# Layer 0's head in another fixed order: a hybrid decoder trunk on one core

## Chip, cores, metric

The kernel runs on one core of one Trainium2 chip. The metric is the device time of one execution in microseconds (us), as the median of several runs. The profile is one further execution, taken by the hardware profiler; its times count from the span's start.

## The reference

Two layers, each a mixing block and an MLP, on 512 positions of width 1024:

```
for l in range(2):
    h = rms_norm(x, norm_mix_g[l])
    proj = h @ w_in[l]                      # 1024 -> 26 groups of 128 columns
    mixed = [diff_attention(...), short_conv(...), rwkv7_time_mix(...)]
    x = x + mixed @ w_out[l]
    h = rms_norm(x, norm_mlp_g[l])
    x = x + square(relu(h @ w_mlp_up[l])) @ w_mlp_down[l]
return rms_norm(x, final_norm_g)
```

with `rms_norm(x, g) = x * rsqrt(mean(x*x) + 1e-6) * g`. Everything is float32.

## The kernel before, in words

**Layout.** Activations lie transposed: `x[j]`, j = 0 to 7, holds 128 channels by 512 positions. A weight group g is 128 output columns; its 1024 rows are eight blocks k of 128 x 128, loaded as halves of four blocks. A product on TensorE (PE) multiplies one block by one 128 x 512 tile into PSUM.

**Three products for one.** For precision each operand is split in a high part (rounded to fp32r) and a low part (the rest). Block k of group g takes three products: high weight by high input, high weight by low input, low weight by high input (`passes`, L685 ff.; all matmuls are issued from L282).

- The high part of input tile j, `ahim` in the profile, is made by ScalarE (ACT) from x[j] and the norm's gain (L420); the text calls it ahi j. Its low part, `alom`, is made by VectorE (DVE) after it (L421): alo j.
- The high part of a weight half, `whi` or `whi_s`, is a cast on ACT from the loaded tile `raw` (L671). The low part, `wlo` or `wlo_s`, is a subtraction on DVE or GpSimd (POOL) (L683). `raw` has three buffers; the next load waits for the low part of the tile that lay there.
- The norm works on x itself: the first square goes straight into the accumulator `accm` (L429), the later squares `sqm` (L433, ACT, two buffers) are added to it by DVE (L436): square j, sum j. PE then adds over the partitions (`pssm`, called pss here), DVE and POOL take the inverse root, PE spreads it over the partitions (`prbm`, called prb), ACT copies it to `rsm` (L789). The projections are scaled by `rsm` only after their products.

**The head.** In layer 0 the first three groups, 24, 18 and 15, go through the eight blocks together: for each k three products of each group, nine in all, so that PE can begin when input tile 0 and the first blocks are there. Their first halves are loaded and cast in two pieces (one block, then three). After the 72 products of the head come the other groups one by one, group 0 first. Group 24 feeds the rates (`rates`, L804 ff.): scaled by `rsm` (`pwa`), mixed with the position before (`dwa`, `zwa`), tanh (`th`), split in parts (`tw`, `to`), and then multiplied by small weights (`lkt`, `lvt` from the load `lor`) into `pw`, three times; a DVE scan (L835) takes each `pw` out of PSUM.

**What sets the order.** Nothing is scheduled by the compiler: `drive` walks through a string per layer, `ORDER[l]`. Each letter is a generator, and a letter with a number takes so many of its steps; a step issues one instruction or a few. So the string fixes the order on every engine and on every DMA queue. The letters of the changed stretch are: d the loads (SyncE's queue, SP, but for two), e ahi and alo, q squares and sums, w casts to high parts, x low parts on DVE, y low parts on POOL, m products, k constants (among them the cast `exact` of the load `ex`), n the norm from pss to `rsm`, g the rates. `SLOTS` fixes in the same way which buffer each new tile takes; the load `ex` takes its turn in the two buffers of the squares.

Of the kernel before, what the change touches and what calls it, by code (L numbers as in the profile page):

```python
# [56 lines left out]
      "xyxyyxxxyyxxyyxyxxyxyyxyyyyyyxxxyyyxyxyyyyyyyxxxxxyyyyyyyyyyxyxyxxxxyyxxyy")  # L57

ORDER = (
         "g d10 e w e m w x m w m x m2 x m q m3 w x e m w e m2 x m2 w x m d2 e m3 d3 e m3 q2 m3 d q2 e q e q d5 w2 e w x e x d4 m3 q2 x d2 m2 e m2 e "  # L60
         "d m2 q e m2 q m4 e k q m3 e m3 q2 m3 k4 q e k m5 k3 m7 n3 w y m2 w2 m2 x d2 m3 n2 g y m6 k g d k m3 k g2 m k2 m4 g m g m2 w m2 g m2 g x m3 "
         "d g5 m2 g2 m3 A w g m4 g y A2 d m4 A2 m3 g m2 g2 w m y h m6 R g3 d R2 g R m4 w m2 g m g4 y R m3 R d m R m2 A2 m h R2 m w m3 A x d A m2 A m "
         "R m A2 m R3 m2 A2 m2 R3 m w x m A m2 A m5 d m4 R3 w m4 x R2 m4 d m4 g2 R2 w A m A y A7 m2 d m A R4 A5 m11 w y R2 m A2 m d A2 m A m r A2 R r "
         "A m4 A3 m w y R2 r h A3 R9 r d r2 m3 A2 h2 R3 m A m A3 R m2 r A2 m2 r R3 m4 w m A3 m2 R r2 y R m5 A2 r2 R2 d A m A2 r m A m2 A r m3 r3 A B "
# [1543 lines left out]
```

## Time and profile before

| | us |
|---|---|
| median of 3 runs | 1241.8 |
| lowest, highest | 1240.58, 1242.72 |
| span of the profiled execution | 1241.5 |

The page gives the busy time of each engine over the span, the waits and the chain of work that ended last; the time line gives instructions with their start, duration, engine, line, output and inputs, and in brackets the idle time of the engine ahead of it and what ended that. The page names no time of the profiled execution but its span, from the first to the last instruction.

### The profile page before, as it was taken

What the parts mean: (1) busy time and instruction counts of PE and PEld (TensorE: products, weight loads), DVE (VectorE), ACT (ScalarE), POOL (GpSimd) and SP (SyncE); (2) the same over time, 40 slices, a digit from 0 to 9 for tenths busy, and PEclk for the clock granted to TensorE, in tenths of its full rate; (3) what the DMA queues carried; (4) which work ended last, traced back from release to release, by engine and by line L of the source; (5) the groups of instructions that cost most, each with busy time, mean ns of one, the idle gap of its engine ahead of it and who ended that gap; (6) DMA issues with size and microseconds to landing.
All of it is one profiled execution on the core that took longest, in us unless ns stands there. A gap on an engine that the chain in (4) does not pass through costs nothing.

```text
span 1241.5 us, 24974 instructions
## 1 busy us (share of the span) xinstructions
PE 1230.0 (99%) x9492; PEld 1055.0 (85%) x9492; DVE 912.1 (73%) x1776; ACT 675.0 (54%) x1410; POOL 368.0 (30%) x457
## 2 busy tenths in 40 slices
PE   9999999999999999999999999999999999999997
PEld 6888888888899998989887888888888999998987
DVE  6787888868767676765766777887687767676753
ACT  6785655548445454544464657464583445454542
POOL 1263637342311111111026355464231211111111
PEclk9999999999999999999999999999999999999999
DMA  6523324142433333321235244332433333333121
GB/s 216 163 87 99 105 96 111 53 153 85 136 102 98 107 94 106 99 85 44 69 106 164 79 118 119 89 83 73 158 102 120 102 102 98 107 94 107 55 68 68
DMA packets 84695, 127.90 MB, mean 103 GB/s; under 512 B 21472, under 2 KB 25568, under 8 KB 84576
## 3 DMA queue, kind: packets, MB, share of 16 engines
q1 hardware_dynamic: 83568, 125.64, 33.1%
q8 instruction: 74, 1.21, 0.4%
q10 hardware_dynamic: 1008, 0.68, 0.2%
q14 instruction: 45, 0.37, 0.1%
HBM read 117.11 MB, written 9.18 MB: 102 GB/s over the span
## 4 chain that ended last, share of the span: by engine, by line
PE 93%; ACT 2%; DVE 2%; DMA 1%; POOL 1%; issue 1%; ACTq 0%; POOLq 0%; DVEq 0%
PE dn L282 25%; PE pj L282 20%; PE pa L282 11%; PE po L282 8%; PE up L282 7%; PE pb L282 6%; PE dnF L282 4%; PE pc L282 3%; PE sc L282 1%; DMA raw<-wts 1%; PE ptt L287 1%; PE pg L282 1%; PE pyy L282 1%; PE pzw L282 1%; PE pst L282 1%
## 5 line engine op out<-in xcount | busy, mean ns | idle before, releaser
L1392 POOL TENSOR_TENSOR ml<-m,mh 128x512 fp32r<-128x512 f32 x64 | 108.9, 1716 | 481.0 <-ACT mh L1391 340.6
L344 ACT CAST whi<-raw 128x512 fp32r<-128x512 f32 x142 | 87.4, 619 | 162.4 <-PE dn L282 152.8
L282 PE MATMUL dn<-mh,whi 128*128 128x512 f32 x448 | 174.8, 390 | 0.1
L282 PE MATMUL dn<-ml,whi 128*128 128x512 f32 x448 | 174.6, 390 | 0.0
L282 PE MATMUL dn<-mh,wlo 128*128 128x512 f32 x448 | 174.5, 390 | 0.0
L683 POOL TENSOR_TENSOR wlo<-raw,whi 128x512 fp32r<-128x512 f32 x84 | 111.0, 1321 | 213.1 <-ACT whi L671 175.4
L282 PE MATMUL pj<-ahim,whi 128*128 128x512 f32 x392 | 156.7, 400 | 0.4 <-DVE vf L1278 0.4
L282 PE MATMUL pj<-ahim,wlo 128*128 128x512 f32 x392 | 156.4, 399 | 0.0
L282 PE MATMUL pj<-alom,whi 128*128 128x512 f32 x392 | 155.9, 398 | 0.0
L1516 DVE TENSOR_TENSOR x<-dn,x 128x512 f32<-128x512 f32 x112 | 77.3, 690 | 103.1 <-PE dn L282 103.1
L671 ACT CAST whi<-raw 128x512 fp32r<-128x512 f32 x142 | 87.6, 617 | 83.3 <-PE pj L282 25.1
L345 DVE TENSOR_TENSOR wlo<-raw,whi 128x512 fp32r<-128x512 f32 x142 | 115.0, 811 | 11.2 <-ACT whi L344 8.3
L282 PEld LDWEIGHTS dn<-mh,wlo 128*128 128x128 f32 x448 | 84.1, 188 | 17.8
L282 PEld LDWEIGHTS dn<-mh,whi 128*128 128x128 f32 x448 | 84.1, 188 | 17.5 <-issue 0.4
L282 PEld LDWEIGHTS dn<-ml,whi 128*128 128x128 f32 x448 | 84.1, 188 | 16.7
L1455 ACT CAST shi_p<-s 128x512 fp32r<-128x512 f32 x96 | 59.6, 621 | 70.1 <-PE pa L282 55.1
L282 PEld LDWEIGHTS pj<-ahim,whi 128*128 128x128 f32 x392 | 73.9, 188 | 14.1 <-issue 0.8
L282 PEld LDWEIGHTS pj<-alom,whi 128*128 128x128 f32 x392 | 73.9, 188 | 13.9 <-issue 0.5
L282 PEld LDWEIGHTS pj<-ahim,wlo 128*128 128x128 f32 x392 | 73.9, 188 | 13.8 <-issue 0.2
L1456 DVE TENSOR_TENSOR slo_p<-s,shi_p 128x512 fp32r<-128x512 f32 x96 | 67.9, 708 | 19.7 <-ACT shi_p L1455 17.2
L282 PE MATMUL pa<-tlo,shi_p 128*128 128x256 f32 x288 | 81.3, 282 | 0.0
L282 PE MATMUL pa<-thi,shi_p 128*128 128x256 f32 x288 | 81.2, 282 | 0.0
(414 smaller groups left out, 3208.1 us busy)
## 6 DMA issues: line engine op xcount, KB each, us to landing
raw<-wts SPq DMA_DIRECT2D x389, 256.0 KB, 2.7
qs<-dqhi SPq DMA_DIRECT2D x24, 128.0 KB, 3.7
ks<-dkhi SPq DMA_DIRECT2D x24, 128.0 KB, 3.7
x<-xT SPq DMA_DIRECT2D x8, 256.0 KB, 4.6
dqhi<-qhi SPq DMA_DIRECT2D x6, 256.0 KB, 3.4
dqlo<-qlo SPq DMA_DIRECT2D x6, 256.0 KB, 3.4
dkhi<-khi SPq DMA_DIRECT2D x6, 256.0 KB, 2.7
dklo<-klo SPq DMA_DIRECT2D x6, 256.0 KB, 3.5
```

Source lines behind the costliest of these rows:

```text
L282: ins = nc.tensor.matmul(*a, **k)
L287: ins = nc.tensor.transpose(*a, **k)
L344: act.copy(hi[:, :n], raw[:, :n])
L345: (pool if a and lean[0] else dve).tensor_tensor(lo[:, :n], raw[:, :n], hi[:, :n].bitcast(F32), ALU.subtract)
L671: yield act.copy(hi[:, k0:k1], raw[:, k0:k1])
L683: yield eng.tensor_tensor(lo[:, k0:k1], raw[:, k0:k1], hi[:, k0:k1].bitcast(F32), ALU.subtract)
L1392: pool.tensor_tensor(lo, m, hi.bitcast(F32), ALU.subtract)
L1455: act.copy(hi, src)
L1456: dve.tensor_tensor(lo, src, hi.bitcast(F32), ALU.subtract)
L1516: dve.tensor_tensor(x[j], pt, x[j], ALU.add)
```

## The change

Two lines of the order of layer 0 are changed. The number of steps of each letter in them is the same before and after, and all lines behind them are untouched.

```diff
-"g d10 e w e m w x m w m x m2 x m q m3 w x e m w e m2 x m2 w x m d2 e m3 d3 e m3 q2 m3 d q2 e q e q d5 w2 e w x e x d4 m3 q2 x d2 m2 e m2 e "
-"d m2 q e m2 q m4 e k q m3 e m3 q2 m3 k4 q e k m5 k3 m7 n3 w y m2 w2 m2 x d2 m3 n2 g y m6 k g d k m3 k g2 m k2 m4 g m g m2 w m2 g m2 g x m3 "
+"g d10 e w e m w x m w m x m2 x m e m3 w e x m3 w x m2 w x m d2 e m3 d3 e q e m3 e q2 m3 d6 w e x e q w x w x e2 q2 d4 m3 q d2 m2 e m2 q "
+"d m2 e q m2 e m4 q k q m3 e m3 q2 m3 k4 q2 k m5 k3 m13 n3 w y m2 w2 m3 x d2 m3 n2 g y k g d k m2 k g2 m k2 m4 g m g m2 w m2 g m2 g x m3 "
```

Written out by engine:

- ACT, before: square 0, cast 24, ahi1, casts 18 and 15 (second pieces), ahi2, squares 1 and 2, ahi3, square 3, casts of the second halves of 24 and 18, ahi4, that of 15, square 4, ahi5, square 5, ahi6, exact, square 6, ahi7, square 7.
- ACT, after: ahi1, casts 24, 18 and 15 (second pieces), ahi2, square 0, ahi3, square 1, cast of the second half of 24, ahi4, square 2, those of 18 and 15, ahi5, square 3, ahi6, square 4, ahi7, square 5, exact, squares 6 and 7.
- DVE, after: alo1 ahead of the low part of 24's second piece; alo2, alo3, sum 1, low part of 24's second half, alo4, low parts of 18's and 15's, alo5, sums 2 and 3, alo6, sums 4 and 5, alo7, sum 6, four small constants, sum 7. Before, a sum stood behind each of alo2 to alo6 or close to it, and alo7 behind sum 7.
- PE: the products keep their order. pss stands six products later among them, and eight products instead of seven lie between pss and prb; so prb stands seven products later, and fewer products lie between prb and the first product into `pw`.
- The order on POOL and on SP's queue is the same.

## The prediction

> **What bounds the kernel now.** I read the page first, for the engine that never rests. TensorE (PE) is busy 99% of the span at full clock, and the chain that ended last is 93% PE. Time can only move where PE waits.
>
> ```profile
> span 1241.5 us, 24974 instructions
> PE 1230.0 (99%) x9492; PEld 1055.0 (85%) x9492; DVE 912.1 (73%) x1776; ACT 675.0 (54%) x1410; POOL 368.0 (30%) x457
> PE 93%; ACT 2%; DVE 2%; DMA 1%; POOL 1%; issue 1%; ACTq 0%; POOLq 0%; DVEq 0%
> ```
>
> The change touches the first 27 us, so the next views are the busy time by stretches (duration, then PE, PEld, DVE, ACT, POOL), and the chain in order of time.
>
> ```profile
> 0.00:22.00 22.00, 19.62 (x75) 12.74 (x75) 14.81 (x33) 15.68 (x30) 1.22 (x7) 1.00 0.82 268
> 22.00:45.00 23.00, 23.00 (x112) 18.95 (x112) 17.23 (x31) 17.41 (x30) 8.79 (x12) 1.00 0.33 104
> ```
>
> ```profile
> 6.57 0.53 ACT accm L429
> ...
> 8.83 0.56 DVE wlo_s L683
> ...
> 9.41 4.32 DMA raw<-wts
> ...
> 25.45 7.54 PE pj L282 x33
> ```
>
> PE idles some 2.4 us before 22 us and not at all from 22 to 45. The chain gives PE's pace: 7.54 / 33 = 0.228 us from product to product. It also shows what delays the start: the first square (accm), and a weight load that went out only at 9.41, when DVE had finished the low part of an earlier tile. The time line has PE's waits:
>
> ```profile
> 7.19 0.40 PE L282 MATMUL pj<-ahim,wlo_s 128*128 128x512 f32 x1
> 8.18 0.50 PE L282 MATMUL pj<-ahim,whi_s 128*128 128x512 f32 x1 [0.59 <-ACT ahim L420]
> 8.97 0.50 PE L282 MATMUL pj<-alom,whi_s 128*128 128x512 f32 x1 [0.29 <-DVE alom L421]
> 9.30 0.40 PE L282 MATMUL pj<-ahim,wlo_s 128*128 128x512 f32 x1
> 15.05 0.50 PE L282 MATMUL pj<-ahim,whi_s 128*128 128x512 f32 x1
> 20.25 0.39 PE L282 MATMUL pj<-ahim,whi_s 128*128 128x512 f32 x1
> 21.61 0.95 PE L282 MATMUL pssm<-ones,accm 128*128 128x1 f32 x8
> ```
>
> **First part, input tile 1 ahead of its square.** ACT and DVE around it:
>
> ```profile
> 6.48 0.63 ACT L429 ACTIVATE accm<-x 128x512 f32<-128x512 f32 x1
> 7.01 0.50 ACT L671 CAST whi_s<-raw 128x384 fp32r<-128x384 f32 x1
> 7.41 0.72 ACT L420 ACTIVATE ahim<-x,prm 128x512 fp32r<-128x512 f32 x1
> 8.16 0.75 DVE L421 SCALAR_TENSOR_TENSOR alom<-x,prm,ahim 128x512 fp32r<-128x512 f32 x1
> ```
>
> ahi1 takes the square's place: 6.48 + 0.72 = 7.20 (if tile 1 has landed by 6.48; ACT was busy, so the row can't show it, and at the worst ahi1 starts at 7.41 as now and the step gains nothing). Each instruction here starts some 0.1 before the end of the one ahead, so the cast behind it runs 7.10 to 7.60, and PE's first product of tile 1 starts at 7.64 instead of 8.18. alo1 follows ahi1: 7.23 to 7.98, so the second product starts at 8.03; the weight's low part follows 7.88 to 8.44, so the third starts at 8.49 against 9.30. That is 0.8 gained; I keep 0.75, since a product after a wait took 0.33, not 0.23, until the next.
>
> **Second part, tiles 4 to 7 ahead of squares and of late casts.** From 15.05 to 20.25 PE issued 18 products, 4.10 at its pace, in 5.20: 1.1 of waits, on alo4, the low part of weight 15's second half and alo5. ahi4 stood behind the cast that waited for the load of 9.41; the change puts ahi4 and alo4 before it. With tile 4 done by about 13.7 and the rest below, no product of tiles 4 to 6 finds its operand missing. So PE could be at the norm's sums (pss) 0.75 + 1.1 = 1.85 earlier. The change puts six products ahead of pss, 6 x 0.228 = 1.37: in the order of before pss would stand at 21.61 + 1.37 = 22.98, and PE now arrives at 22.98 - 1.85 = 21.1.
>
> **Third part, the sums.** pss needs all eight squares added by DVE, and these have been pushed back. Rows for the paces, and for the wait that now decides:
>
> ```profile
> 17.02 0.63 ACT L433 ACTIVATE sqm<-x 128x512 f32<-128x512 f32 x1 [0.37 <-DVE accm L436]
> 17.51 0.74 DVE L421 SCALAR_TENSOR_TENSOR alom<-x,prm,ahim 128x512 fp32r<-128x512 f32 x1
> 18.17 0.68 DVE L436 TENSOR_TENSOR accm<-accm,sqm 128x512 f32<-128x512 f32 x1
> 18.77 0.74 DVE L421 SCALAR_TENSOR_TENSOR alom<-x,prm,ahim 128x512 fp32r<-128x512 f32 x1
> 13.75 0.62 ACT L671 CAST whi_s<-raw 128x512 fp32r<-128x512 f32 x1 [1.46 <-DMA raw<-wts]
> 20.04 0.16 DVE L445 TENSOR_SCALAR drv<-prm 128x11 f32<-128x11 f32 x1
> 20.40 0.69 DVE L436 TENSOR_TENSOR accm<-accm,sqm 128x512 f32<-128x512 f32 x1
> ```
>
> DVE takes 0.66 from a low part to the next instruction and 0.60 from a sum. The squares share two buffers, so a square waits for the sum two allocations back: the 0.37 above.
>
> The load of 9.41 waits for the low part of 8.83, ended at 9.39; that now ends at 8.90 (two low parts of 0.56, started 0.47 apart, behind the one that ends at 8.44), so the cast of 13.75 starts at about 13.25. The next load's cast follows to 14.6, ahi5 to 15.2, alo5 15.25 to 16.0. Only then come sum 2 (15.9) and sum 3 (16.5 to 17.2). Square 4 has to wait for sum 3's buffer: 17.25 to 17.87. Sum 4 runs 17.9 to 18.6, square 5 in the same buffer 18.6 to 19.25, sum 5 19.27 to 19.95, alo7 from 19.87, sum 6 from 20.53, four small instructions (20.40 - 20.04 = 0.36), sum 7 from 21.5 to 22.2. pss then starts at 22.25, and PE, there since 21.1, waits 1.1: of the 1.85, 0.73 is left. If the load keeps its 13.75, everything is 0.45 later (pss 22.7); if it takes only the 2.7 of the last row below, ACT is what its cast waits for, 0.25 earlier (22.0).
>
> SP's queue has a part. ex shares the squares' buffers and now waits for sum 2, 16.6 instead of 13.79; queued behind it are four constant loads and the next weights. The cast named exact waits for ex, and squares 6 and 7 stand behind exact.
>
> ```profile
> 13.79 0.33 SPq L648 DMA_DIRECT2D ex<-cst  x1
> 16.47 18.09 SPq L629 DMA_DIRECT2D raw<-wts  x8
> 21.14 1.88 ACT L671 CAST whi<-raw 128x512 fp32r<-128x512 f32 x3 [0.77 <-DMA raw<-wts]
> ```
>
> ```profile
> ex<-cst SPq DMA_DIRECT2D x1, 128.0 KB, 3.5
> raw<-wts SPq DMA_DIRECT2D x1, 256.0 KB, 2.7
> ```
>
> A load from an empty queue took 2.7 (the one issued at 23.40), ex itself, behind others, 3.5. With 2.7 exact starts at 19.35, square 6 ends at 20.4, before sum 6 wants it: no cost. With 3.5 square 6 ends at 21.2, sum 6 starts at 21.23 and pss at 22.95. I take 2.7, as all loads ahead of ex are out by then. The Trainium skill ("DMA: Bandwidth & Descriptors", Anatomy of one DMA) puts a transfer at about 2.0 us plus its bytes over 436 GB/s; by that, an estimate for another issuing path, ex lands at 18.9 and costs nothing, while the row of 3.5 would add 0.7. The next weights go out at about 18.4 instead of 16.47, 1.9 later; their first cast ends at 23.7 at the latest, and PE wants it six products behind pss, at 22.25 + 0.95 + 1.37 = 24.6: hidden.
>
> **Fourth part, what hangs on the sums.** The root, its broadcast (prb), the scaled group 24 and its tanh form one chain of latency over DVE, POOL, PE and ACT, in the same order as before. Its start moves from 21.61 to 22.25: D = 0.64 later, all of it. PE reaches its end sooner than before, for the change leaves seven products fewer behind prb.
>
> ```profile
> 22.94 1.31 POOL L369 TENSOR_TENSOR rrm<-rsx,ones 128x4 f32<-128x4 f32 x1 [21.19 <-DVE rsx L365]
> 31.93 0.56 DVE L823 TENSOR_TENSOR lvt<-lor,lkt 128x384 fp32r<-128x384 f32 x1
> 33.06 0.39 PE L282 MATMUL pw<-to,lvt 128*128 128x512 f32 x1
> 35.75 1.22 DVE L835 TENSOR_TENSOR_SCAN lw<-cst,pw 128x512 f32<-128x512 uint8 x1 [0.41 <-ACT pw L831]
> 37.41 0.39 PE L282 MATMUL pw<-tw,lkt 128*128 128x512 f32 x1
> ```
>
> Two places decide. lvt ended at 32.49, 0.57 ahead of PE's product of 33.06; a product starts some 0.06 behind its operand, so 0.51 is slack and PE moves by at least D - 0.51 = +0.13. The scan of 35.75 ended at 36.97 and frees the PSUM buffer for the product of 37.41: slack 0.38, so PE moves by at least D - 0.38 = +0.26. Behind these PE's pace rules again (no idle to 45 us), and the rest of the kernel, 97% of it, just moves by that. Of 1.85 us gained at the head, 1.1 is lost at pss and the rest at pw. The break-even is a pss at 21.99.
>
> **The sum.** 1241.5 + 0.26 = 1241.8 for a profiled execution. The median of before's runs, 1241.8, is 0.3 above its span, so I predict 1242.1. The bounds: pss from 22.0 to 22.7 by the load, to 23.4 if ex is slow as well: 0.0 to +1.4 on PE.
>
> **The rivals.**
> *Part of the head's gain stays.* If sum 7 were done by 21.0, PE would run through pss at 21.1 and D would be -0.5; at pw PE then moves by D - 0.38 = -0.88, the most that the chain behind the sums lets through: 1240.9. For it speaks that PE really waited 2.4 us in this stretch; against it that square 4 cannot start before sum 3, and sum 3 now stands behind alo5. Chance 0.17.
> *Slower, by ex.* ex's wait for sum 2 holds SP's queue. It decides once ex lands later than about 19.5, that is 2.9 after its issue; with its own 3.5, D is 1.34 and PE moves by +0.96: 1242.8. With the late weight load too, 1243.2. Chance 0.20.
> *Nothing moves.* The later stages are set by waits among DVE, ACT and POOL that don't follow a quarter of a microsecond, and absorb it: 1241.8. For it: 7% of the chain that ended last is not PE. Chance 0.13.
>
> **How the numbers follow.** The forecast has the remaining 0.50. It and "nothing moves" lie within 0.4 of before; the two others reach 1240.9 and 1243.2. The range takes both in, the lower end by another 0.7 because the runs of before lie up to 1.2 from their median and the faster case has no margin: 1240.2 to 1243.4. 0.2% is 2.5 us, about what a measurement of this kernel can tell from no change. Even the whole waiting time of the head, 2.4, is less; only an effect further on that I don't see would go beyond. So faster 0.04, same 0.91, slower 0.05.
>
> **What would show it.** In the changed profile PE's first product of tile 1 starts near 7.6; the waits at tile 4 and 5 are gone; one wait of about 1 us stands ahead of pss, released by DVE's accm, with pss near 22.25; ex is issued near 16.6; there are waits of 0.1 to 0.5 at the products pw. If pss starts without a wait, or before 22.0, my chain of squares is wrong and the time falls below before; if ACT's exact is what square 6 waits for and pss is past 22.9, the slower rival holds.

## The result, and the profile after

| us | before | after |
|---|---|---|
| median of 18 runs each | 1242.76 | 1244.11 |
| lowest, highest | 1240.58, 1246.35 | 1242.96, 1249.77 |
| span of the profiled execution | 1241.5 | 1241.7 |

The changed kernel takes 1.0016 times as long (95% interval 1.0010 to 1.0022), so it is slower by 1.35 us by the medians. That is within the 0.2% of the prediction's bound, but above 1242.1 and above the upper end of its range, 1243.4. Both spans lie well within what one execution differs from the next, so they don't rank the two kernels; the first 55 us have to be read piece by piece.

The page of after has the same totals as that of before, but for the chain, where DVE now has 3% and PE 92%:

```profile
span 1241.7 us, 24974 instructions
PE 1229.5 (99%) x9492; PEld 1055.3 (85%) x9492; DVE 912.6 (73%) x1776; ACT 675.7 (54%) x1410; POOL 367.6 (30%) x457
PE 92%; DVE 3%; ACT 2%; POOL 1%; DMA 1%; issue 1%; ACTq 0%; POOLq 0%; DVEq 0%
```

By stretches (duration, then busy time of PE, PEld, DVE, ACT, POOL):

```profile
0.00:22.00 22.00, 20.03 (x79) 13.83 (x80) 15.17 (x34) 15.12 (x28) 1.22 (x7) 1.00 0.78 260
22.00:45.00 23.00, 21.91 (x106) 17.77 (x106) 16.88 (x29) 18.02 (x30) 8.53 (x12) 1.00 0.35 112
```

Before, PE idled 2.38 us ahead of 22 us and not at all from 22 to 45. Now it idles 1.97 and 1.09. The time line of PE shows where:

```profile
7.32 0.39 PE L282 MATMUL pj<-ahim,whi_s 128*128 128x512 f32 x1
16.41 0.39 PE L282 MATMUL pj<-ahim,whi_s 128*128 128x512 f32 x1
20.50 0.40 PE L282 MATMUL pj<-ahim,wlo_s 128*128 128x512 f32 x1
21.64 1.05 PE L282 MATMUL pssm<-ones,accm 128*128 128x1 f32 x8 [0.75 <-DVE accm L436]
31.19 0.39 PE L282 MATMUL pj<-ahim,whi 128*128 128x512 f32 x1
32.55 0.47 PE L282 MATMUL pw<-tw,lkt 128*128 128x512 f32 x1 [0.97 <-DVE tw L817]
33.14 0.47 PE L282 MATMUL pw<-to,lvt 128*128 128x512 f32 x1
52.83 0.47 PE L282 MATMUL pj<-ahim,whi 128*128 128x512 f32 x1 [0.42 <-DVE vf L1278]
```

The first product of tile 1 starts at 7.32 instead of 8.18, and no wait is left at tiles 4 and 5. Product for product PE runs up to 2.5 us ahead of before (16.41 against the row of 18.88 below: 2.47). Then it waits at pss (21.64 - 20.50 - 0.23 = 0.91 beyond its pace), and pss starts at 21.64 against 21.61. Six more products lie behind PE there than before, so a part of the gain is still left: the last product ahead of the first pair into `pw` starts at 31.19, where before it started at 32.59, 1.40 earlier. At that pair PE waits twice, where before had no wait, and this takes the rest and 0.2 more.

The row of 52.83 is a mark for all kernels below: the product behind `vf`, the end of the stretch that the change touches. Before it stood at 52.59. Three rows of before:

```profile
18.88 0.39 PE L282 MATMUL pj<-ahim,whi_s 128*128 128x512 f32 x1
...
32.59 0.40 PE L282 MATMUL pj<-ahim,whi 128*128 128x512 f32 x1
...
52.59 0.47 PE L282 MATMUL pj<-ahim,whi 128*128 128x512 f32 x1 [0.42 <-DVE vf L1278]
```

So PE is 0.24 later there. The chain of waits shows what holds the sums, and what follows them:

```profile
15.97 0.70 DVE accm L436
16.69 0.64 ACT sqm L433
17.36 0.70 DVE accm L436
18.09 0.64 ACT sqm L433
18.75 0.69 DVE accm L436
...
21.00 0.60 DVE accm L436
21.64 1.05 PE pssm L282 x8
...
27.73 0.45 issue
28.18 0.76 DVE zwa L801
```

From 15.97 a square waits for the sum that frees its buffer, and the next sum waits for that square, twice over: the ladder that the prediction had. New is the "issue" of 0.45 ahead of `zwa`: DVE had nothing left to wait for, and did nothing for 0.45 us.

### The profile page after: what moved, and what is told of

The parts are those of the page before. It is cut to its first block, busy times and chain, and to the rows that moved or that the text cites. A ratio compares the mean times of both kernels' runs of the same rounds, so it can differ in the third digit from the quotient of the medians.

```text
span 1241.7 us, 24974 instructions
## 1 busy us (share of the span) xinstructions
PE 1229.5 (99%) x9492; PEld 1055.3 (85%) x9492; DVE 912.6 (73%) x1776; ACT 675.7 (54%) x1410; POOL 367.6 (30%) x457
## 3 DMA queue, kind: packets, MB, share of 16 engines
q8 instruction: 74, 1.21, 0.4%
## 4 chain that ended last, share of the span: by engine, by line
PE 92%; DVE 3%; ACT 2%; POOL 1%; DMA 1%; issue 1%; ACTq 0%; POOLq 0%; DVEq 0%
PE dn L282 25%; PE pj L282 19%; PE pa L282 11%; PE po L282 8%; PE up L282 7%; PE pb L282 6%; PE dnF L282 4%; PE pc L282 3%; PE sc L282 1%; PE ptt L287 1%; PE pg L282 1%; DMA raw<-wts 1%; PE pyy L282 1%; PE pzw L282 1%; PE pst L282 1%
## 5 line engine op out<-in xcount | busy, mean ns | idle before, releaser
L282 PEld LDWEIGHTS dn<-ml,whi 128*128 128x128 f32 x448 | 84.1, 188 | 16.6
```

The costliest lines, as they stand in the source:

```text
L282: ins = nc.tensor.matmul(*a, **k)
```

## The experiments

Each was timed in five rounds beside before on the same chip, unless it says one execution; the first row is the result above. The column pss has the start of pss in the profile (before: 21.61). "Mark" is the start of the product behind `vf` (before: 52.59); D is the shift of the end of `lvt` (before: 32.49).

| kernel | ratio (95%) | median, us | pss | D | mark - 52.59 |
|---|---|---|---|---|---|
| after, first profile | 1.0016 (1.0010 to 1.0022) | 1244.11 | 21.64 | +0.50 | +0.24 |
| before again | 1.0003 (0.9994 to 1.0011) | 1242.80 | 21.42 | -0.20 | -0.19 |
| after again | 1.0019 (1.0010 to 1.0028) | 1244.78 | 22.54 | +1.40 | +1.13 |
| after, third time | one execution | 1243.38 | 21.75 | +0.60 | +0.34 |
| head only | 1.0027 (1.0018 to 1.0037) | 1245.92 | 21.75 | +1.95 | +1.68 |
| norm only | 1.0008 (0.9999 to 1.0017) | 1244.08 | 23.00 | +1.38 | +1.10 |
| after, one memset more | 1.0003 (0.9995 to 1.0012) | 1243.48 | 22.30 | +0.74 | +0.47 |
| before, one memset more | one execution | 1243.11 | 21.85 | +0.64 | +0.38 |
| head only, filled | 1.0019 (1.0007 to 1.0030) | 1244.90 | 22.35 | +0.87 | +0.61 |
| after, filled | 1.0012 (1.0003 to 1.0021) | 1244.20 | 22.40 | +1.17 | +0.90 |
| after, own square buffers | 1.0000 (0.9991 to 1.0009) | 1242.78 | 22.00 | +0.49 | +0.22 |
| tile 1 only | 0.9988 (0.9979 to 0.9997) | 1241.74 | 20.41 | -1.21 | -1.20 |

In every row with a D above zero PE's shift at the mark is D - 0.27, within 0.03. That is the rule of the prediction's fourth part, with a slack of 0.27 where it had 0.38. So a profile is judged by its D; what is to be found is what sets D, and what the times hold besides.

**The two kernels again.** Neither is edited.

> The kernel before, unchanged, timed against itself and profiled once more. In the first profile of before input tile 1 could start only at 7.41 us and the cast of weight 15's first block at 6.27; in the profile of after the same cast, with the same queue order ahead of it, ran at 5.04. Theory A (loads vary, and before gains from early ones): a second profile of before with that cast near 5.0 has its sums (pss) near 20.6 instead of 21.61, and a span near 1240.5; the ratio against itself is 1.000 within 0.0008. Theory B (the two profiles of before and after, 1241.5 and 1241.7, are typical): pss again near 21.6 and a span near 1241.5.

> The changed kernel, profiled once more and timed. Both theories: slower than before by 0.1 to 0.2%. Theory A: PE waits again at pss (about 1 us, for the last sum) and again at the two products into pw (0.5 to 1.7 us together), whatever the loads do, and PE passes the third pw product 0.2 to 1 us later than in the first profile of before (37.41). Theory B: the cost of 1.4 to 2 us lies later, between 45 and 290 us, and changes from profile to profile.

> The changed kernel profiled a third time. PE behind the second pw product at D - 0.38 + 0.1 later than in the first profile of before, D being the end of lvt against 32.49: 0.2 to 1.2 by the landing of the first loads.

In after's second profile the first loads came later, and the whole head with them:

```profile
9.51 4.59 DMA raw<-wts
...
22.54 1.05 PE pssm L282 x8
```

Tile 1 landed at 4.84 in the first profile of after, at 6.12 in this one and at 4.90 in the third; in the two profiles of before it was 6.05 and 5.94. The issue times were the same within 0.01. The weights behind tile 1 come late with it. Before suffers by this too: in its first profile ACT waits for such a weight, and square 0 and ahi1 stand behind that cast.

```profile
6.27 0.30 ACT L671 CAST whi_s<-raw 128x128 fp32r<-128x128 f32 x1 [1.36 <-DMA raw<-wts]
```

All four profiles with the old head (both of before, "norm only" and "before, one memset more") had late loads; of the nine with a changed head five had early ones. So no profile shows before with early loads, and whether the order has a part in when they land isn't shown. With the late loads D is 1.40, and the mark moves by 1.13 against before's first profile and by 53.72 - 52.40 = 1.32 against its second, both of which had the late loads too. So the +0.24 of the first profile compares early loads with late ones, a lucky draw for the new kernel; 1.13 to 1.32 is the like-for-like figure for late loads.

**One half of the change alone.** "Head only" is after with the six products put back behind the norm (against after), "norm only" is before with them ahead of it (against before):

```diff
-"d m2 e q m2 e m4 q k q m3 e m3 q2 m3 k4 q2 k m5 k3 m13 n3 w y m2 w2 m3 x d2 m3 n2 g y k g d k m2 k g2 m k2 m4 g m g m2 w m2 g m2 g x m3 "
+"d m2 e q m2 e m4 q k q m3 e m3 q2 m3 k4 q2 k m5 k3 m7 n3 w y m2 w2 m2 x d2 m3 n2 g y m6 k g d k m3 k g2 m k2 m4 g m g m2 w m2 g m2 g x m3 "
```

```diff
-"d m2 q e m2 q m4 e k q m3 e m3 q2 m3 k4 q e k m5 k3 m7 n3 w y m2 w2 m2 x d2 m3 n2 g y m6 k g d k m3 k g2 m k2 m4 g m g m2 w m2 g m2 g x m3 "
+"d m2 q e m2 q m4 e k q m3 e m3 q2 m3 k4 q e k m5 k3 m13 n3 w y m2 w2 m3 x d2 m3 n2 g y k g d k m2 k g2 m k2 m4 g m g m2 w m2 g m2 g x m3 "
```

> Only the first half of the change: tiles ahead of squares and casts; the norm's sums stay at their old place among the products. Theory A: the last sum still ends at 21.6 (profile of after), so PE waits some 2.4 us at pss but has its six products behind it to cover the chain to pw: no waits at pw, pss 0.0 to 0.3 later than in before, and a time like that of after within 0.5 us: ratio 1.0005 to 1.0015. Rival R (the six products ahead of the sums are what costs): ratio 1.000 or below, 0.9995.

> Only the second half: six products ahead of the norm's sums, with the head in its old order. pss stands 1.37 later (22.98 by the first profile of before), PE has nothing to wait for there, but the chain behind the sums starts 1.37 later and at pw the slacks of 0.51 and 0.38 are used up: Theory A: waits of about 0.9 at pw, PE some 1.0 later from there on, ratio 1.0008. Rival R: the same or more, 1.0008 to 1.0016, the whole of the change's cost.

In "norm only" PE doesn't wait at pss, which simply stands 1.37 later in its stream (23.00, with pss at 21.61 before), and the chain behind the sums is as much later: D = 1.38, mark +1.10. The time agrees, 1.0008 as expected, but its interval just takes in 1. So the six products are no gain where they don't fill a wait. "Head only" came out slower than either expectation, 1.0027. PE reaches pss without the six products, and waits:

```profile
19.18 0.39 PE L282 MATMUL pj<-ahim,wlo_s 128*128 128x512 f32 x1
21.75 1.33 PE L282 MATMUL pssm<-ones,accm 128*128 128x1 f32 x8 [2.18 <-DVE accm L436]
23.50 0.63 PE L282 MATMUL pj<-alom,whi_s 128*128 128x512 f32 x1
23.93 0.63 PE L282 MATMUL pj<-ahim,wlo_s 128*128 128x512 f32 x1
...
25.94 1.05 PE L282 MATMUL prbm<-cst,rrm 128*128 128x128 f32 x8
```

```profile
22.00:24.00 2.00, 2.00 (x11) 1.81 (x11) 0.82 (x4) 1.61 (x3) 0.56 (x1) 0.59 0.37 140
24.00:26.00 2.00, 2.00 (x7) 1.57 (x6) 0.34 (x1) 0.24 (x1) 2.00 (x3) 0.56 0.29 68
26.00:28.00 2.00, 2.00 (x15) 1.78 (x14) 0.35 (x1) 0.69 (x2) 1.89 (x4) 1.00 0.60 192
```

Behind the wait a product takes 0.43 to the next instead of 0.23. The granted clock (third figure from the right) tells why: 0.59 and 0.56 between 22 and 26, full speed on both sides. At half speed for x us of 2, the mean is 1 - x/4; that gives 1.64 and 1.76, together 3.4 us at half speed. From pss to prb it takes 4.19 instead of before's 2.69 (24.30 - 21.61), with seven products between in both, so it costs 1.5, and D is 1.95. The prediction has no such cost. Of the 12 executions of this kernel 8 show a mean granted clock of 0.996 or less. Of 30 executions of after it is 5, of the 96 of before whose clock is on record 2. That mean is a coarse sign: each of the 13 profiles ends with 4 to 8 us at half clock, and the profiled execution of "head only", with its 3.4 us near pss, has a mean of 0.997.

The Trainium skill ("TensorE: Matmul & The Clock Gate", Part 1) says that the clock is judged over free-running windows of about 3.4 us and drops to half after an idle one. The length agrees: 3.4 us here. But the wait was 2.57 from start to start, shorter than the window, with eight small products of pss behind it. So by this profile the window need not be idle throughout.

**The wait filled.** Products whose result nobody reads were put ahead of pss, into the bank that the warming products at the start use: 11 in "head only", 5 in after:

```diff
                 pt = psum("rp", 4, f"pss{key}")
+                for _ in range(11 if l == 0 else 0):
+                    pe.matmul(idle, parts[24][0][:, 0], acts[0][0], start=True, stop=True)
```

> The new head with the sums at their old place (head_only), and eleven products into an unused PSUM bank in front of pss, 2.5 us by PE's pace: work in the time in which PE waited 2.57 for the last sum. Theory C (TensorE's clock is halved for a stretch after that wait; head_only's profile shows 3.41 us at 0.5, and 8 of its 12 executions had a mean granted clock of 0.996 or less against none of 35 of before): no stretch at half clock near 22 us, all executions at 0.997 or more, ratio 1.0007 to 1.0012 instead of 1.0027. Rival (the clock is not the cause, the late sums are): ratio 1.0022 to 1.003.

> The changed kernel with five products into an unused PSUM bank ahead of pss, 1.14 us by PE's pace, in the time of its wait of 1.15. If a part of the change's cost is a halved clock after that wait (5 of 29 executions of after had a mean granted clock of 0.996 or less, 3 of 82 of before): all or nearly all executions at 0.997 or more and ratio 0.0002 to 0.0004 below that of after, 1.0013 to 1.0016. Rival: clocks and ratio as in after, 1.0016 to 1.0019.

Filled, "head only" runs at full clock through pss:

```profile
19.85 2.66 PE L282 MATMUL idle<-ahim,whi_s 128*128 128x512 f32 x11
22.35 0.95 PE L282 MATMUL pssm<-ones,accm 128*128 128x1 f32 x8
```

```profile
20.00:24.00 4.00, 4.00 (x24) 3.43 (x23) 2.83 (x12) 1.67 (x4) 0.33 (x1) 1.00 0.77 260
24.00:28.00 4.00, 4.00 (x23) 3.39 (x22) 1.62 (x5) 2.23 (x5) 3.90 (x5) 1.00 0.40 112
```

Its D falls from 1.95 to 0.87, though pss starts 0.6 later. Its time is another matter: 1.0019, between the 1.0007 to 1.0012 of the theory and the 1.0022 of the rival, and not below after's 1.0016 to 1.0019. 3 of 12 executions are at 0.996 or less, where the theory had none. The profiled execution has a stretch at half clock elsewhere, in layer 1:

```profile
762.00:766.00 4.00, 2.30 (x43) 1.69 (x41) 3.90 (x8) 2.02 (x5) 1.46 (x4) 1.00 0.43 131
766.00:773.00 7.00, 7.00 (x116) 6.03 (x117) 3.16 (x10) 3.45 (x8) 1.03 (x2) 0.51 0.01 2
```

PE was busy for 2.30 of 4 us, and then ran 7 us at half speed. In the other 12 profiles it is busy for 3.9 to 4.0 of these 4 us, at full clock throughout. So part of what these times hold is chance at other places. One thing more: in every other kernel an execution's time is its span plus 1.74 to 1.87; in "after, filled" it is 1.76 to 3.68, median 2.7, and in two executions of "head only, filled" 2.4 and 3.9. By spans alone, "after, filled" has a median of 1241.8 against 1241.2 for the executions of before beside it, +0.6, where after had 1242.3 (first) and 1243.0 (again) against 1240.9 in the runs of before beside it again. "Head only, filled" has 1242.75, "head only" 1244.1. So the spans are 0.5 to 1.4 shorter with the filling, though measured on different chips, and no execution of "after, filled" was at 0.996 or less. That after pays for a halved clock is not shown by this. What lies outside the span I can't explain: with eleven products instead of five the median is 1.8 as in the other kernels, so it isn't simply the filling.

**The pause ahead of `zwa`.** In the first profile of after DVE's wait for `dwa` was over at 27.73, and `zwa` started at 28.18. The new head has one wait instruction more in DVE's stream. If the pause hangs on where an instruction stands in it, one more instruction far ahead of it moves it. Into both kernels went a memset of a constant's unused column, 0.06 us long:

```diff
-    dve.memset(ones1, 1.0)
+    dve.memset(ones1, 1.0); dve.memset(fixed[:, 3:4], 0.0)
```

> The changed kernel with one more tiny DVE instruction (a memset of one unused column) right at the start; nothing else. In all three profiles with the changed head DVE starts zwa 0.51 to 0.53 after dwa's end, in all three with the old head 0.10; the new head gives DVE's program one more wait instruction ahead of it. Theory P (DVE's sequencer pauses some 0.45 at a fixed place of its program, and the new head has pushed that place in front of zwa): with one instruction more the pause falls elsewhere, zwa starts 0.10 after dwa, the end of lvt lies 10.9 behind pss instead of 11.35, PE is 0.4 earlier behind pw than in after; ratio 1.0012 to 1.0016. Rival (zwa waits for data, for instance POOL's memsets): 0.5 and 11.35 as before, ratio 1.0017 to 1.0019.

> The kernel before with the same extra memset. Theory P: the pause now lies in front of zwa: 0.5 behind dwa instead of 0.10, lvt's end 11.35 behind pss instead of 10.88. Rival: 0.10 and 10.88.

The pause goes away in after and appears in before. The rows of `zwa` in after, in after with the memset, in before and in before with the memset, in this order:

```profile
28.18 0.75 DVE L801 SCALAR_TENSOR_TENSOR zwa<-pwa,prm,dwa 128x512 f32<-128x512 f32 x1 [1.01 <-POOL lee L825]
```

```profile
28.41 0.75 DVE L801 SCALAR_TENSOR_TENSOR zwa<-pwa,prm,dwa 128x512 f32<-128x512 f32 x1 [0.61 <-ACT dwa L800]
```

```profile
27.67 0.76 DVE L801 SCALAR_TENSOR_TENSOR zwa<-pwa,prm,dwa 128x512 f32<-128x512 f32 x1 [0.61 <-ACT dwa L800]
```

```profile
28.32 0.75 DVE L801 SCALAR_TENSOR_TENSOR zwa<-pwa,prm,dwa 128x512 f32<-128x512 f32 x1 [1.02 <-POOL lee L825]
```

The idle time ahead of `zwa` is 0.61 or 1.01. The releaser in the brackets is inferred, and where the pause is, the wrong one: POOL's `lee` is no input of `zwa`, and in after with the memset it ran from 28.13 to 28.54, past the start of `zwa`. All 13 profiles agree on the place. With the pause, `zwa` is the 64th of DVE's recorded instructions, waits included, in all seven profiles; without it, it is the 63rd (four profiles), the 65th or the 66th. From pss to the end of `lvt` before takes 10.88, after 11.35, after with the memset 10.92, before with the memset 11.28. The time of after with the memset is 1.0003 of before (0.9995 to 1.0012), lower than the 1.0012 to 1.0016 that was expected; by the medians it is +0.8, where after had +1.35 and +2.1. What DVE does in the pause no row shows.

**Squares that don't wait for sums.** To test the ladder, squares 3 to 7 of the changed kernel got a buffer each, out of five that are used only later; `ex` then waits for sum 1 alone:

```diff
-         "wp/sq 101011010101010 "
+         "wp/sq 1010101010 "
...
-                sq = wp.tile([P, S], F32, tag="sq", bufs=2, name=f"sqm{l}_{j}")
+                if l or j < 3:
+                    sq = wp.tile([P, S], F32, tag="sq", bufs=2, name=f"sqm{l}_{j}")
+                else:
+                    sq = ready["mp"].tile([P, S], F32, tag=("bon", "rt", "yi", "ee", "dx")[j - 3], name=f"sqm{l}_{j}")
...
+            ready["mp"] = mp
```

> The changed kernel with squares 3 to 7 in five buffers of their own (tiles that are free until later), so that no square waits for a sum and the load ex waits only for sum 1. DVE's program gets two more wait instructions ahead of zwa. Theory (the sums are late because square 4 waits for sum 3 and square 5 for sum 4): sum 7 ends 0.6 to 0.9 earlier than in after, pss at 20.7 to 21.0 with early loads and 21.6 to 21.9 with late ones, PE's wait there 0.2 to 0.5 instead of 1.15; and, if the pause before zwa hangs on the number of instructions ahead, zwa 0.10 behind dwa and lvt's end 10.9 behind pss. Both together: PE behind pw 1.0 to 1.3 earlier than in after, ratio 0.9995 to 1.0007. Rival (DVE's own order, sums behind alo5, sets the sums): pss within 0.3 of after's, ratio 1.0012 or more.

In its profile tile 1 landed late (6.02), tile 2 at 9.45, the latest of all profiles. Still PE hardly waits at pss:

```profile
21.61 0.39 PE L282 MATMUL pj<-ahim,wlo_s 128*128 128x512 f32 x1
22.00 1.05 PE L282 MATMUL pssm<-ones,accm 128*128 128x1 f32 x8
```

PE waits 22.00 - 21.61 - 0.23 = 0.16 at pss, where after had 0.91. PE comes 0.21 later to pss than in after's profile with late loads, and yet pss is 0.54 earlier. At 22.00 it is just later than the 21.6 to 21.9 expected for late loads. What the ladder costs is seen without the loads in the stretch from alo5 to sum 7 on DVE, first in after, then here:

```profile
14.52 0.74 DVE L421 SCALAR_TENSOR_TENSOR alom<-x,prm,ahim 128x512 fp32r<-128x512 f32 x1
20.90 0.69 DVE L436 TENSOR_TENSOR accm<-accm,sqm 128x512 f32<-128x512 f32 x1
```

```profile
15.60 0.74 DVE L421 SCALAR_TENSOR_TENSOR alom<-x,prm,ahim 128x512 fp32r<-128x512 f32 x1
21.26 0.69 DVE L439 TENSOR_TENSOR accm<-accm,sqm 128x512 f32<-128x512 f32 x1
```

It takes 6.38 in after (6.40 in its second profile) and 5.66 here: 0.7 is the ladder, as expected; the 5.66 are DVE's own work behind alo5. The pause is gone here as well; DVE's stream has two wait instructions more. So D, 0.49 instead of 1.40, holds both: 0.54 from pss and 0.37 from the shorter chain behind it. The time is 1.0000 of before, from 0.9991 to 1.0009: the loss is taken back, and no more, and the times don't tell the two apart.

**Tile 1 alone.** Only the first part of the change: ahi1 and alo1 ahead of square 0, which goes behind the first casts; all else as in before.

```diff
-"g d10 e w e m w x m w m x m2 x m q m3 w x e m w e m2 x m2 w x m d2 e m3 d3 e m3 q2 m3 d q2 e q e q d5 w2 e w x e x d4 m3 q2 x d2 m2 e m2 e "
+"g d10 e w e m w x m w m x m2 x m e m3 w e x m3 w x m2 w x m d2 q e m3 d3 e m3 q2 m3 d q2 e q e q d5 w2 e w x e x d4 m3 q2 x d2 m2 e m2 e "
```

> The old order with one move of the new: the parts of input tile 1 go ahead of the first square, and that square follows behind the casts of the first weight pieces. By the rule that PE behind pw moves with the end of the sums: tile 1's products 0.5 to 0.8 earlier, the second-half weight loads 0.4 earlier, the last sum at 20.6 to 20.8, pss at 20.8 to 21.1 and PE behind pw 0.4 to 0.7 earlier than in before: ratio 0.9995, span 1241 or less. Rival: the moved square delays the sums as in the whole change, pss at 21.6 or later: ratio 1.000 or above.

```profile
20.18 0.39 PE L282 MATMUL pj<-ahim,wlo_s 128*128 128x512 f32 x1
20.41 0.95 PE L282 MATMUL pssm<-ones,accm 128*128 128x1 f32 x8
...
51.39 0.47 PE L282 MATMUL pj<-ahim,whi 128*128 128x512 f32 x1 [0.42 <-DVE vf L1278]
```

PE goes through pss without a wait, 1.20 earlier than before, and the mark is 1.20 earlier too: all that PE gained in the head is kept, for the sums are there in time. This profile had early loads (tile 1 at 4.95) and before's had late ones, so the 1.20 is not like for like. The chain behind the sums (pss to the end of `lvt`) takes 10.87, as before. The time, over 11 executions, is 0.9988 of before, the whole interval below 1, 0.96 us less by the medians: better than both kernels of the case.

## Why the prediction missed

It forecast 1242.1, and it was 1244.1. Of these 2.0 us, 0.96 is the base and 1.05 the change. Two steps failed: the base, and the length of the chain behind the sums.

**The base.** The step that failed here is "The median of before's runs, 1241.8, is 0.3 above its span, so I predict 1242.1". The three runs shown were on the low side, 1241.8 where 18 runs gave 1242.76. And the profiled execution's time isn't its span: for after it was 1243.53 with a span of 1241.7, and for all unfilled kernels the time is the span plus 1.74 to 1.87. So by that rule the execution with the span of 1241.5 took about 1243.3, slower than its own median by 0.5. One place where it lost time is far behind the change, in layer 1. There the chain of waits of before goes through a weight load:

```profile
672.73 5.50 DMA raw<-wts
...
682.88 1.15 PE pj L282 x5
```

After's first profile goes through the same load, and so does before's second (5.58 us). In after's second profile the chain there is PE alone, and of the 1.13 that it was behind, 0.05 is left. The first and the second profile of after:

```profile
673.19 5.35 DMA raw<-wts
```

```profile
682.93 1.15 PE pj L282 x5
```

So two spans can differ by a microsecond by a chance in layer 1: this is why after's second span, 1241.5, equals before's first one. I took one span for the middle of the runs, and the 0.3 for what lies around a span.

**First part, tile 1.** Right, with a size that hangs on the loads. With tile 1 there in time its first product came at 7.32 instead of the 7.64 worked out, and the third was 1.52 earlier than before; with tile 1 late, in after's second profile, the first came at 7.74 and the third was 0.70 earlier, against the 0.75 that I kept. Alone this part is worth 0.96 by the times.

**Second part, tiles 4 to 7.** Right: the waits of 1.1 are gone. On its way to pss PE was up to 2.5 ahead of before in the first profile, with early loads, and 1.67 in the second, against 1.85.

**Third part, the sums.** The mechanism is right: sums behind alo5, square 4 behind sum 3, a wait at pss released by `accm`, a part of the head's gain lost there and the rest at `pw`. "pss then starts at 22.25" became 21.64, 21.75 or 22.54, by when the first loads landed. From alo5 to sum 7 the prediction had 15.25 to 21.5, 6.25, and it was 6.38 to 6.40; alo5 itself came at 14.52 in the first profile and at 15.40 in the second. The bounds, 22.0 to 22.7, came from the weight load's row, and the landing of the first tiles was taken as given by one trace. By the prediction's own sign, a pss before 22.0 would mean that the chain of squares is wrong and the time falls. The first profile has 21.64, with the chain of squares as worked out and no fall in the time: the sign took no account of early loads.

**ex.** Issued at 15.93, not 16.6, and landed 1.9 later:

```profile
ex<-cst SPq DMA_DIRECT2D x1, 128.0 KB, 1.9
```

So its cast waited for square 5 on its own engine, not for it, and the rival that had the kernel slower by `ex` falls; the kernel is slower by another way. The formula of the Trainium skill ("DMA: Bandwidth & Descriptors", Anatomy of one DMA), given there for another issuing path, puts 128 KB at some 2.3, an estimate. The 1.9 of this case's trace is nearer to that than to the row of 3.5 or to the 2.7 that I took.

**Fourth part, what hangs on the sums.** "D = 0.64 later, all of it" failed: the step took the chain from pss to `lvt` to be as long as before. It was 0.47 longer, 0.43 of it the pause, which the memset shows to hang on the instruction stream. With early loads the two errors, pss too late by 0.6 and the chain too short by 0.47, nearly cancelled, and the mark moved by 0.24 where 0.26 was forecast: that agreement is luck. With late loads, as in the trace that the prediction was made from, they add up: D is 1.40, and of the 0.87 by which the mark is beyond 0.26, 0.47 is the longer chain, 0.29 the later pss and 0.11 the slack. The rule itself held in every profile with a D above zero, with 0.27 for 0.38.

**The clock.** Not in the prediction at all. Behind a wait at pss the clock was halved in the profile of "head only", where it costs some 1.5, and with the wait filled it was not. For after it is only inferred from 5 of 30 executions with a low mean clock, none of which has a trace; its three profiles have full clock there.

**The rivals.** "Part of the head's gain stays" is what "tile 1 only" does, not this change: its price of 0.88 is close to the 0.96 measured there by coincidence, as it was worked out from the slack at `pw` of another order. "Nothing moves" falls, as the ratio's interval excludes 1 twice.

**What is open.** Like for like the profiles give +1.1 to +1.3 at the mark, the times +1.35 and +2.1. The halved clock and chance in layer 1 can fill the difference, but this isn't settled. Nor is it known why the first loads land at two different times, or what before would gain from early ones.

## What to carry to other kernels

When products are moved ahead of a sum that a long chain hangs on, count the chain's shift, not PE's gain: PE keeps what it gains only as long as the sum, and the end of the chain behind it, are ready when it arrives. Here the part of the change after which the sums were still there in time was worth a microsecond, while the whole cost more than one. Judge an edit of this size by the point where PE's pace rules again, in two profiles or more of each kernel, and take the base from many timed runs rather than from the span of one. A stall without a releaser, or with one that isn't an input, may hang on the place in the instruction stream; one cheap instruction put ahead of it tells.

## What was unexpected of the hardware

- In one profile a wait of 2.57 us at pss, eight tiny products at its end, was followed by 3.4 us at half clock; products took 0.43 instead of 0.23. In another one, after a stretch with PE busy for 2.30 of 4 us, there were 7 us at half clock.
- DVE paused for 0.4 us behind a wait that was over, in front of the 64th of its recorded instructions when that was `zwa`, and a 0.06-us memset far ahead moved the pause away or brought it in.
- Loads issued at the same time landed at two different times from one execution to the next: tile 1 at 4.84 to 4.95 in five profiles, at 5.61 to 6.30 in the eight others.
- In one kernel, with five products into an unused bank, the time outside the span had a median of 2.7 instead of 1.8; with eleven such products it was 1.8.
